# Layer one of a four-layer decoder trunk: VectorE's deferrable work gathered into one list, worked off at three places of each unit

## The chip, the cores and the metric

The kernel runs on one core of a Trainium2 chip. The metric is the device time of one launch in microseconds, lower is better. Five engines work side by side and meet only at semaphores: TensorE (PE; PEld is its weight load), VectorE (DVE), ScalarE (ACT), GpSimd (POOL) and SyncE (SP), which here only issues the weight loads.

## The reference

The input x has 256 positions of 1024 numbers, all float32. Four layers follow one another, each with a mixer of its own: `h = h + rms_norm(mixer(rms_norm(h)))`. The change touches the first, native sparse attention, with 16 query heads, 4 groups of keys, and head width 64:

```python
q, kc, vc, ks, vs, kw, vw, gl, z = split_cols(u @ w_in, A_SPLITS)
kcmp, vcmp = compress(kc, pos_k, w1_k, w2_k), compress(vc, pos_v, w1_v, w2_v)   # gelu(blocks @ w1) @ w2
p_c = masked_softmax(q . kcmp - slope * dist);  o_c = p_c . vcmp    # 15 compressed blocks
p_s = masked_softmax(q . ks   - slope * dist);  o_s = p_s . vs      # top 16 of 4 blocks: all of them
p_w = masked_softmax(q . kw   - slope * dist);  o_w = p_w . vw      # window 512 > 256: all causal keys
o = g_c * o_c + g_s * o_s + g_w * o_w                               # sigmoid gates
return (o * silu(z)) @ w_out
```

With 256 positions the selected and the window branch are both plain causal attention, over different keys and values.

## The kernel before

**Weights.** All weights stream in one order, `seq`, in pieces of up to 512 KB. Each piece is loaded by SP into one of five buffers (`raw`, NS = 5), then split into two float32r parts: a high part (`whi`, a rounded copy by ACT, L133) and a low part (`wlo`, raw minus high, by DVE, L72). A projection is three matmuls per 128 rows: high by high, low of the activations by high, high by low of the weights (L226 to L228). Up to eleven pairs of parts are alive (NH = 11): when the queue's steps are done with a piece, `free` and `advance` let the next piece be split. Below, pieces go by their place in `seq`: 16 and 17 are the first group's queries (called q0), 18 to 25 the compression's w1 (not split), 26 and 27 q1, 28 and 29 z0, 30 and 31 q2, 32 and 33 z1, 34 and 35 q3, 36 and 37 z2, 38 and 39 z3, 40 to 47 the output projection, 48 on the next layer. Here z0 to z3 are the four quarters of the gate path.

**A raw buffer comes free only when its low part is done**, so a low part starts the load five pieces further on.

**Whose order counts.** PE runs in the order of the source throughout. From the compression to the end of the first layer's attention (`st["own"]`), DVE does so too; ACT's order is chosen by the scheduler. In that stretch a low part isn't issued at once: `advance` puts it into `low`, and it is issued by `low_parts(1)` at fixed places, or at the latest when a projection step needs it. Other work that can wait goes through `later(n, f)`: it is issued once n more projection steps have been issued (`plan["count"]`), by `overdue`, which is called after each step.

**The compression.** `compress` does four rounds of eight matmuls, each followed by four steps of q0's projection and, after the first three, `low_parts(1)`. It ends with a cubic and a tanh (`cubic`), then `hidden_t` transposes the hidden values, `second_layer` applies w2 and writes the compressed keys `kc` (L738, L739) and values (L747). Nine steps of q1 stand before `hidden_t`, six after it.

**The units.** `nsa_order` writes 63 places in a row: for each pair of heads p = 0 to 7 (a unit) the front of unit p and the back of unit p-1 in turn. Each unit's places are: `cmp_front` (even p: scores against compressed keys and their reduction L793); `first` (scores of the first 128 queries for both heads, four softmax passes L325 on DVE, then the scaling of the unit before, `scale`, L865 and L871, mixed with five small operations of the compressed branch); `second` (scores of the other 128 queries of head 0, two passes L325); `cmp_back` (odd p); `trans(0)` and `trans(1)` (six transposes L332 each, of unit p-1, copied out by ACT, L172); `finish` (the second queries of head 1, two passes L325); `pvs` (products with the values for unit p-1). After each place `fill` issues projection steps from the queue: two per place up to unit 3, one per place after that; each step is three matmuls. `need(g)` issues steps until group g's queries are there.

The scores sit in two PSUM buffers (`S`, NSB = 2). The second queries of head 0 take the buffer of the first queries of head 0, and so on in turn, so that each score matmul (L846, L847) waits for the DVE pass L325 that read the same buffer before.

**The gate.** `have_z` runs tanh on ACT and then L434 on DVE (`later(6)`), `have_o(p)` calls `go`, which multiplies a quarter of the output by it (L385), and `split` makes its parts (L393, L394) for the output projection.

Of the kernel before, what the change touches and what calls it, by code (L numbers as in the profile page):

```python
# [10 lines left out]
F32 = mybir.dt.float32  # L11
# [4 lines left out]
OP = mybir.AluOpType  # L16
# [7 lines left out]
NH, NS = 11, 5  # L24
LATE, LATEZ, EARLY = -250, -60, 80
NMM, NSB = 3, 2
KO = (0, 4, 1, 5, 2, 6, 3, 7)
X1AT, SUMAT, UAT, T1AT, WARM = 4, 1, 3, 4, 12
POOLED = (6,)
# [8 lines left out]
def trunk(ctx, tc, I, out):  # L38
# [11 lines left out]
    seq = []  # L50
# [11 lines left out]
    for n in "bcd":  # L62
        add(n + "_v", *range(8))
        add(n + "_t", *range(20 if n == "c" else 24))
        add(n + "_o", *range(8))
    st = {"load": 0, "split": 0, "next": 0, "held": 0, "parts": 0, "after": [], "most": len(seq), "own": False}
    raw, parts, low = {}, {}, {}
    waiting = deque()

# [8 lines left out]
    def low_parts(n):  # L78

        for i in sorted(low)[:n]:  # L80
            low.pop(i)()

    def later(n, f):

        if st["own"]:
            waiting.append((plan["count"] + n, f))
        else:
            f()

    def overdue(everything=False):  # L90
        due = [w for w in waiting if everything or w[0] <= plan["count"]]
        for w in due:
            waiting.remove(w)
            w[1]()
        if due:
            overdue(everything)

    def advance(most=len(seq)):
        while True:
# [141 lines left out]
    def pop():  # L241
        fq.popleft()()
        plan["count"] += 1
        overdue()
# [6 lines left out]
    def need(i):  # L251

        while fq and (i not in ready or plan["count"] < ready[i] + 6):
            pop()

    def push_proj(use, q=fq, idx=None):

# [96 lines left out]
    class Gate:  # L354
# [18 lines left out]

        def have_o(self, p):
            self.o.add(p)
            self.go()

        def go(self):
            while self.ready < 4:
# [297 lines left out]
    def keep_q(o, g):  # L677


        for j in range(2):  # L680
            r, other = HALF[j], HALF[1 - j]
            hs = slice(4 * g + j, 4 * g + j + 3, 2)
            hi, sc = t["q"][r, hs, :], cq[r, 2 * g:2 * g + 1]
            with tc.high_priority(offset=EARLY):
                ACT.activation(hi, o[r], AF.Copy, scale=sc)
            later(5, lambda r=r, other=other, hs=hs, hi=hi, sc=sc: DVE.scalar_tensor_tensor(
                t["q"][other, hs, :], o[r], sc, hi.bitcast(F32), op0=OP.mult, op1=OP.subtract))
        ready[g] = plan["count"]

    t = {}  # L690
    W1 = []

    def compress(q, lp):
        if q == 0 and lp == 0:
            t["h"] = ps.tile([128, 256], F32, name="o", bufs=1)
        for kv in range(2):
            PE.matmul(t["h"][64 * kv:64 * kv + 64, :], blkT[:, kv, 4 * q + lp, :], parts[W1[q][kv]][:, lp, :],  # L697
                      start=(q == 0 and lp == 0), stop=(q == 3 and lp == 3))
        if lp == 3:
            free(*W1[q])  # L700
            advance()
        if q == 3 and lp == 3:
            t["q"] = big.tile([128, 16, 256], F32R, name="qT")
            hp = t["h"]
            hid = t["hid"] = work.tile([128, 384], F32, name="P", bufs=8)[:, 0:256]
            ht = work.tile([128, 384], F32, name="P", bufs=8)[:, 0:256]
            ACT.activation(ht, hp, AF.Square)

            def cubic():
                DVE.tensor_scalar(ht, ht, 0.044715, 1.0, op0=OP.mult, op1=OP.add)  # L710
                DVE.tensor_tensor(ht, ht, hp, op=OP.mult)
                ACT.activation(ht, ht, AF.Tanh, scale=math.sqrt(2.0 / math.pi))
                later(3, lambda: DVE.scalar_tensor_tensor(hid, ht, 1.0, hp, op0=OP.add, op1=OP.mult))

            later(1, cubic)
# [16 lines left out]
    def second_layer():  # L732
        kp = ps.tile([128, 512], F32, name="S", bufs=NSB)
        for k in range(2):
            PE.matmul(kp[:, 0:60], w2[:, 0, k].rearrange("p a b -> p (a b)"), t["hk"][:, k, :],
                      start=k == 0, stop=k == 1)
        kp4 = kp[:, 0:60].rearrange("p (g n) -> p g n", g=4)
        ACT.activation(kc[:, :, 0, 0:15], kp4, AF.Copy, scale=0.5)  # L738
        DVE.scalar_tensor_tensor(kc[:, :, 1, 0:15], kp4, 0.5, kc[:, :, 0, 0:15].bitcast(F32), op0=OP.mult,  # L739
                                 op1=OP.subtract)  # L740
        vp = ps.tile([128, 256], F32, name="o", bufs=1)
        for g in range(4):
            for k in range(2):
                PE.matmul(vp[0:60, g * 64:(g + 1) * 64], t["hv"][:, k, g].rearrange("p a b -> p (a b)"),
                          w2[:, 1, k, 0, :], start=k == 0, stop=k == 1)
        for g in range(4):
            DVE.tensor_tensor(vbd[g], vp[0:60, None, g * 64:(g + 1) * 64].to_broadcast([60, 4, 64]),  # L747
                              bm[:, :, None].to_broadcast([60, 4, 64]), op=OP.mult)
# [79 lines left out]
    def nsa_unit(p):  # L828
        g, i = divmod(p, 2)
        t = {}  # L830

        def start():
            need(g)
            t["P"] = {(j, br): work.tile([128, 384], F32, name="P", bufs=8) for j in range(2) for br in range(2)}
            t["l"], t["mx"] = small(8, "la", 3), small(8, "mxa", 3)

        def scores_of(b, js):
            if b == 0:
                start()
            n = 128 * (b + 1)  # L840
            S = {}
            for j in js:
                s = ps.tile([128, 512], F32, name="S", bufs=NSB)
                s = s[:, 0:2 * n].rearrange("p (a n) -> p a n", a=2)
                q = qT[:, 2 * p + j, b * 128:(b + 1) * 128]
                PE.matmul(s, q, KH[:, g, :, 0:n], start=True, stop=False)  # L846
                PE.matmul(s, q, KL[g // 2][:, g % 2, :, 0:n], start=False, stop=True)  # L847
                S[j] = s
            for j in js:
                for br in range(2):  # L850
                    x = (j * 2 + br) * 2 + b
                    softmax(S[j][:, br, :], causal[i], SLA[4 * g + j], 128 * b, 128 * b + n, t["P"][j, br],
                            t["mx"][:, x:x + 1], t["l"][:, x:x + 1])

        def finish():
            scores_of(1, (1,))
            low_parts(1)
            SCALE.append(scale())

        def scale():  # L860
            l = t["l"]
            gv = bass.AP(tensor=gate.tensor, offset=gate.offset + 16 + 2 * p,
                         ap=[list(gate.ap[0]), [1, 2], [16, 2], [48, 2]])
            l4 = l.rearrange("p (j r b) -> p j r b", j=2, r=2)
            ops = [lambda: DVE.reciprocal(l, l), lambda: DVE.tensor_tensor(l4, l4, gv, op=OP.mult)]  # L865
            for br in range(2):
                for j in range(2):
                    x = (j * 2 + br) * 2
                    for b in range(2):
                        P = t["P"][j, br][:, 128 * b:128 * b + 128 * (b + 1)]  # L870
                        ops.append(lambda P=P, x=x + b: DVE.tensor_scalar(P, P, l[:, x:x + 1], None, op0=OP.mult))  # L871
            return ops

        def trans(br):
            t["PT", br] = [transpose_p(t["P"][j, br], "a") for j in range(2)]

        def pv(br):
            if br == 0:
                t["o"] = ps.tile([128, 256], F32, name="o", bufs=1)
            o = t["o"]  # L880
            pv_pair(o, t["PT", br], v, (br * 256 + g * 64,) * 2, br == 0, False)

        def pvs():
            pv(0)
            pv(1)
            o = t["o"]
            for j in range(2):
                PE.matmul(o[64 * j:64 * j + 64, :], vbd[g][:, 2 * i + j, :], PTC[g], start=False, stop=True)
            evac(ga.oT[:, p, :], o, "a")
            ga.have_o(p)  # L890

        def first():
            scores_of(0, (0, 1))
            mixed(*(x.pop(0) for x in (SCALE, CHALF) if x))

        def second():
            scores_of(1, (0,))
            if CHALF:
                mixed(CHALF.pop(0))
            low_parts(1)  # L900

        front = [first, second, finish]
        back = [lambda: trans(0), lambda: trans(1), pvs]
        return front, back

    def nsa_order():
        units = [nsa_unit(p) for p in range(8)] + [([lambda: mixed(SCALE.pop()), *[lambda: None] * 2], None)]
        order = []
        for p in range(9):
            f, b = units[p][0], units[p - 1][1] if p else [lambda: None] * 3  # L910
            if p < 8 and p % 2 == 0:
                order.append(lambda p=p: cmp_front(p // 2))
            order += f[:2]
# [4 lines left out]
                order.append(ga.open)  # L918
        return order

    gh = run(nsa_order(), ga)
    low_parts(len(seq))
    st["own"] = False
    own.close()
# [328 lines left out]
```

## Time and profile before

| | |
|---|---|
| median of 3 runs | 579.8 us (578.29 to 580.72) |
| the profiled execution | 579.91 us, span 578.2 us |
| granted TensorE clock, mean | 0.995 |
| PE busy | 559.3 us, 97% |
| DVE busy | 418.6 us, 72% |
| ACT busy | 335.0 us, 58% |
| the chain that ended last | PE 80%, DVE 9%, issue 5% |

The profile shows one execution. Times in its rows run from the start of the span. A row of the timeline has its start, its length, the engine, the line, the operation, what it writes and reads, and in brackets how long the engine stood idle before it and who released it. A PE matmul's length is a model: back-to-back matmuls start 0.12 us apart and show 0.28. L72's 1.22 us on DVE likewise overlaps its neighbour by some 0.08, so that it takes 1.14 of the engine's time. The units stand between 71 and 158 us.

### The profile page before, as it was taken

Reading aid. Unit: us, or ns where it says so; the run is one execution under the profiler, and the core shown is the slowest. Engines: PE = TensorE matmul, PEld = TensorE weight load, DVE = VectorE, ACT = ScalarE, POOL = GpSimd, SP = SyncE. Lnnn points to the kernel's source line nnn. Section 1 sums busy time; section 2 is a strip of 40 time slices with the busy share of each in tenths; the row PEclk is TensorE's granted clock in tenths of the full one; section 3 lists DMA queues with packets and bytes.
Section 4 is the critical chain, followed back from the end, with each engine's and each line's share of the span. In section 5 each row is a group of like instructions: output and inputs, shape, how many; then the busy total and the mean of one; then the engine's idle time right before and its main releaser. Section 6 shows DMA issues by size and latency. Waiting matters only on the chain.

```text
span 578.2 us, 10454 instructions
## 1 busy us (share of the span) xinstructions
PE 559.3 (97%) x3930; PEld 495.3 (86%) x3930; DVE 418.6 (72%) x927; ACT 335.0 (58%) x719; POOL 41.9 (7%) x89
## 2 busy tenths in 40 slices
PE   7999989999999999999999999999999999999995
PEld 6997878777788799999988789999987898899984
DVE  5883696898857886777965887758548878788632
ACT  6742678788825466567643474757524855666410
POOL 1900000000101100000410100000001000000000
PEclk9999989999999999999999999999999999999999
DMA  9774632322444596443451577443525784332012
GB/s 294 259 246 152 249 110 75 129 91 86 144 154 147 177 332 210 147 147 110 146 158 62 183 270 275 150 143 117 176 73 183 257 289 140 120 108 73 2 37 73
DMA packets 27779, 90.96 MB, mean 157 GB/s; under 512 B 4560, under 2 KB 5200, under 8 KB 27728
## 3 DMA queue, kind: packets, MB, share of 16 engines
q1 hardware_dynamic: 26144, 86.09, 44.2%
q10 hardware_dynamic: 1584, 4.20, 2.3%
q8 instruction: 31, 0.51, 0.4%
q14 instruction: 20, 0.16, 0.1%
HBM read 89.22 MB, written 1.05 MB: 156 GB/s over the span
## 4 chain that ended last, share of the span: by engine, by line
PE 80%; DVE 9%; issue 5%; ACT 2%; POOL 1%; DMA 1%; SPq 0%; POOLq 0%; DVEq 0%; ACTq 0%
PE mm L226 15%; PE mm L227 14%; PE mm L228 14%; PE mm L293 7%; PE mm L292 7%; PE mm L291 7%; DVE wlo L72 4%; PE S L342 3%; PE pt L332 3%; PE o L348 2%; PE o L697 1%; DVE P L325 1%; PE pt L214 1%; DMA h<-in_x_dram 1%; ACT whi L133 1%
## 5 line engine op out<-in xcount | busy, mean ns | idle before, releaser
L226 PE MATMUL mm<-uth,whi 128*128 128x256 f32 x736 | 217.9, 296 | 0.0
L72 DVE TENSOR_TENSOR wlo<-raw,whi 128x1024 fp32r<-128x1024 f32 (+1 forms) x153 | 182.0, 1206 | 41.6 <-ACT whi L133 41.1
L227 PE MATMUL mm<-utl,whi 128*128 128x256 f32 x736 | 208.1, 283 | 0.0
L228 PE MATMUL mm<-uth,wlo 128*128 128x256 f32 x736 | 208.1, 283 | 0.0
L133 ACT ACTIVATE whi<-raw 128x1024 fp32r<-128x1024 f32 (+1 forms) x153 | 156.9, 1044 | 65.9 <-PE mm L227 33.2
L226 PEld LDWEIGHTS mm<-uth,whi 128*128 128x128 f32 x736 | 140.8, 191 | 14.2 <-issue 13.3
L227 PEld LDWEIGHTS mm<-utl,whi 128*128 128x128 f32 x736 | 141.0, 192 | 0.9
L228 PEld LDWEIGHTS mm<-uth,wlo 128*128 128x128 f32 x736 | 140.7, 191 | 0.0
L291 PE MATMUL mm<-whi,qT 128*128 128x512 f32 x128 | 50.4, 394 | 0.0
L292 PE MATMUL mm<-whi,kT 128*128 128x512 f32 x128 | 49.9, 390 | 0.0
L293 PE MATMUL mm<-wlo,qT 128*128 128x512 f32 x128 | 49.9, 390 | 0.0
L291 PE MATMUL mm<-whi,uth 128*128 128x512 f32 (+1 forms) x112 | 42.5, 380 | 0.0
L293 PE MATMUL mm<-wlo,uth 128*128 128x512 f32 (+1 forms) x112 | 42.1, 376 | 0.0
L292 PE MATMUL mm<-whi,utl 128*128 128x512 f32 (+1 forms) x112 | 42.0, 375 | 0.0
L327 ACT ACTIVATE P<-P,mxa 128x128 f32<-128x128 f32 (+1 forms) x64 | 28.4, 446 | 10.6 <-DVE mxa L325 10.5
L325 DVE CUSTOM_DVE_ANT_0 P<-S,mask 128x128 f32<-128x128 f32 (+1 forms) x96 | 29.1, 352 | 7.4 <-PE S L847 5.1
L456 ACT ACTIVATE junk<-mm 128x512 bf16<-128x512 f32 x16 | 9.5, 595 | 42.7 <-PE mm L293 42.7
L332 PE MATMUL pt<-ident,P 128*128 128x128 f32 x180 | 28.3, 280 | 1.7 <-ACT PT L172 0.8
L172 ACT ACTIVATE PT<-pt 128x384 f32<-128x384 f32 x58 | 26.1, 482 | 4.1 <-PE pt L332 3.7
L293 PEld LDWEIGHTS mm<-wlo,qT 128*128 128x128 f32 x128 | 24.0, 188 | 5.0
L291 PEld LDWEIGHTS mm<-whi,qT 128*128 128x128 f32 x128 | 24.1, 188 | 4.7
L292 PEld LDWEIGHTS mm<-whi,kT 128*128 128x128 f32 x128 | 24.1, 188 | 4.7
(206 smaller groups left out, 748.5 us busy)
## 6 DMA issues: line engine op xcount, KB each, us to landing
raw<-in_a_t_dram SPq DMA_DIRECT2D x24, 512.0 KB, 4.4
raw<-in_b_t_dram SPq DMA_DIRECT2D x24, 512.0 KB, 5.0
raw<-in_d_t_dram SPq DMA_DIRECT2D x24, 512.0 KB, 4.6
raw<-in_c_t_dram SPq DMA_DIRECT2D x20, 512.0 KB, 5.6
raw<-in_w_dram SPq DMA_DIRECT2D x8, 512.0 KB, 4.8
raw<-in_a_o_dram SPq DMA_DIRECT2D x8, 512.0 KB, 3.4
raw<-in_b_v_dram SPq DMA_DIRECT2D x8, 512.0 KB, 5.9
raw<-in_b_o_dram SPq DMA_DIRECT2D x8, 512.0 KB, 3.5
```

Of the source, the lines that this page charges most:

```text
L72: lo_of = (POOL if on_pool else DVE).tensor_tensor(lo, t, hi.bitcast(F32), op=OP.subtract)
L133: ACT.activation(hi, t, AF.Copy)
L172: ACT.activation(dst, src, AF.Copy)
L226: PE.matmul(o, sh, mh, start=first, stop=False)
L227: PE.matmul(o, sh, ml, start=False, stop=False)
L228: PE.matmul(o, sl, mh, start=False, stop=last)
L291: PE.matmul(o, sh, wh[:, j, c0:c1], start=k == 0, stop=False)
L292: PE.matmul(o, sl, wh[:, j, c0:c1], start=False, stop=False)
L293: PE.matmul(o, sh, wl[:, j, c0:c1], start=False, stop=k == 7)
L325: DVE.tensor_tensor_reduce(out=P[:, c0:c1], in0=S, in1=mask[:, c0:c1], scale=-slope, scalar=BIG, op0=OP.add, op1=OP.min, accum_out=mx)
L327: ACT.activation(P[:, c0:c1], P[:, c0:c1], AF.Exp, bias=mx, scale=-1.0, accum_out=l)
L332: PE.transpose(pt[:, i, :], P[:, i * 128:(i + 1) * 128], ident)
```

## The change

While the units run, `overdue` issues nothing any more. What is due and the low parts are issued by a new function, `chores(us)`, at three places of each unit: in `trans(0)` (after its transposes and their copies; budget 2.3), in `trans(1)` (likewise; 1.6) and in `finish` (after its two passes L325; 1.2). It takes what is due first, oldest first, at 0.7 each, then low parts at 1.15 each, until the budget is used up or nothing is left; the last item may overrun the budget. Unit 0 has no back, and calls the first two at the same places. `low_parts(1)` goes from `second` and `finish`. `need(g)` now also issues what waits under group g (its queries' low parts L686), and `have_o` calls `go` through `later(2)`. Two more low parts are issued in the compression: one after the tanh in `cubic`, one after L739 in `second_layer`. No computation is added or taken away.

```diff
+U0, U1, U2 = 2.3, 1.6, 1.2
...
-    def later(n, f):
+    def later(n, f, tag=None):
         if st["own"]:
-            waiting.append((plan["count"] + n, f))
+            waiting.append((plan["count"] + n, f, tag))
...
-        due = [w for w in waiting if everything or w[0] <= plan["count"]]
+        due = [w for w in waiting if everything or w[0] <= plan["count"] and not st["units"]]
...
+    def chores(us):
+        while us > 0:
+            due = [w for w in waiting if w[0] <= plan["count"]]
+            if due:
+                waiting.remove(due[0])
+                due[0][1]()
+                us -= 0.7
+            elif low:
+                low_parts(1)
+                us -= 1.15
+            else:
+                return
...
     def need(i):
         while fq and (i not in ready or plan["count"] < ready[i] + 6):
             pop()
+        for w in [w for w in waiting if w[2] == i]:
+            waiting.remove(w)
+            w[1]()
...
         def have_o(self, p):
             self.o.add(p)
-            self.go()
+            later(2, self.go)
...
             later(5, lambda r=r, other=other, hs=hs, hi=hi, sc=sc: DVE.scalar_tensor_tensor(
-                t["q"][other, hs, :], o[r], sc, hi.bitcast(F32), op0=OP.mult, op1=OP.subtract))
+                t["q"][other, hs, :], o[r], sc, hi.bitcast(F32), op0=OP.mult, op1=OP.subtract), g)
...
                 ACT.activation(ht, ht, AF.Tanh, scale=math.sqrt(2.0 / math.pi))
+                low_parts(1)
                 later(3, lambda: DVE.scalar_tensor_tensor(hid, ht, 1.0, hp, op0=OP.add, op1=OP.mult))
...
                                  op1=OP.subtract)
+        low_parts(1)
         vp = ps.tile([128, 256], F32, name="o", bufs=1)
...
         def finish():
             scores_of(1, (1,))
-            low_parts(1)
+            chores(U2)
             SCALE.append(scale())
...
         def trans(br):
             t["PT", br] = [transpose_p(t["P"][j, br], "a") for j in range(2)]
+            chores((U0, U1)[br])
...
         def second():
             scores_of(1, (0,))
             if CHALF:
                 mixed(CHALF.pop(0))
-            low_parts(1)
...
-            f, b = units[p][0], units[p - 1][1] if p else [lambda: None] * 3
+            f, b = units[p][0], units[p - 1][1] if p else [lambda: chores(U0), lambda: chores(U1), lambda: None]
...
+    st["units"] = True
     gh = run(nsa_order(), ga)
+    st["units"] = False
```

## Rows read from the trace of the kernel before

**Rows 1.** Windows: length, then busy time of PE, PEld, DVE, ACT, POOL; granted clock; DMA.

```profile
70.00:80.00 10.00, 7.62 (x57) 7.02 (x56) 9.65 (x36) 6.37 (x18) 0.00 (x0) 1.00 0.28 96
80.00:90.00 10.00, 9.52 (x66) 8.69 (x68) 8.02 (x32) 8.36 (x27) 0.00 (x0) 0.83 0.37 129
...
81.20:84.50 3.30, 3.00 (x13) 2.54 (x12) 3.23 (x19) 2.21 (x7) 0.00 (x0) 0.50 0.47 159
```

**Rows 2.** Waits from 71 to 158 us: who waited for whom, total, times, longest.

```profile
DVE P L325 <- PE S L847: 5.1, 6, 1.9
DVE cs L793 <- PE S L789: 4.8, 3, 2.5
PE S L846 <- DVE mxa L325: 4.3, 5, 2.1
...
PEld pt L332 <- ACT PT L172: 2.4, 7, 0.6
PEld pt L332 <- DVE P L871: 2.3, 8, 0.3
```

**Rows 3.** Timeline of PE around the start of unit 1.

```profile
77.77 0.28 PE L847 MATMUL S<-tu,qT 128*128 128x256 f32 x1
80.18 0.36 PE L846 MATMUL S<-kT,qT 128*128 128x256 f32 x1 [2.13 <-DVE mxa L325]
...
81.74 0.77 PE L846 MATMUL S<-kT,qT 128*128 128x512 f32 x1 [0.30 <-DVE mxa L325]
```

**Rows 4.** Timeline of DVE, unit 0 to the first pass of unit 1.

```profile
71.31 1.21 DVE L72 TENSOR_TENSOR wlo<-raw,whi 128x1024 fp32r<-128x1024 f32 x1
72.44 0.28 DVE L325 CUSTOM_DVE_ANT_0 P<-S,mask 128x128 f32<-128x128 f32 x1
...
76.46 1.22 DVE L72 TENSOR_TENSOR wlo<-raw,whi 128x1024 fp32r<-128x1024 f32 x1
77.71 1.51 DVE L686 SCALAR_TENSOR_TENSOR qT<-mm,cq,qT 64x512 fp32r<-64x512 f32 x2
79.26 0.42 DVE L325 CUSTOM_DVE_ANT_0 P<-S,mask 128x256 f32<-128x256 f32 x1
...
79.95 1.22 DVE L72 TENSOR_TENSOR wlo<-raw,whi 128x1024 fp32r<-128x1024 f32 x1
81.09 0.28 DVE L325 CUSTOM_DVE_ANT_0 P<-S,mask 128x128 f32<-128x128 f32 x1
```

**Rows 5.** Groups of DVE's instructions from 71 to 158 us, shapes apart.

```profile
L72 DVE TENSOR_TENSOR wlo<-raw,whi 128x1024 fp32r<-128x1024 f32 x17 | 20.7, 1219 | 0.0
```

**Rows 6.** Waits of SP's own queue from 71 to 158 us.

```profile
SPq L112 <- DVE wlo L72: 89.8, 18, 14.1
```

**Rows 7.** Timeline of DVE at the end of the compression.

```profile
64.27 0.42 DVE L713 SCALAR_TENSOR_TENSOR P<-P,o 128x256 f32<-128x256 f32 x1 [1.14 <-ACT P L712]
...
66.27 1.23 DVE L72 TENSOR_TENSOR wlo<-raw,whi 128x1024 fp32r<-128x1024 f32 x1
67.52 0.28 DVE L724 COPY P<-pt 128x120 f32<-128x120 f32 x1
...
69.66 1.41 DVE L747 TENSOR_TENSOR v<-o,bm 60x256 f32<-60x256 f32 x4 [0.63 <-PE o L744]
```

**Rows 8.** Timeline of DVE, end of unit 2 and first pass of unit 3.

```profile
103.27 1.22 DVE L72 TENSOR_TENSOR wlo<-raw,whi 128x1024 fp32r<-128x1024 f32 x1
104.41 0.68 DVE L385 SCALAR_TENSOR_TENSOR oT<-oT,zw 128x512 f32<-128x512 f32 x1
105.01 0.28 DVE L325 CUSTOM_DVE_ANT_0 P<-S,mask 128x128 f32<-128x128 f32 x1
```

**Rows 9.** Timeline of PE, the second queries' scores of units 3 and 5.

```profile
105.66 0.47 PE L846 MATMUL S<-kT,qT 128*128 128x512 f32 x1 [0.80 <-DVE mxa L325]
...
125.76 0.47 PE L846 MATMUL S<-kT,qT 128*128 128x512 f32 x1 [0.62 <-DVE mxa L325]
```

**Rows 10.** Timeline of ACT in unit 5.

```profile
127.36 1.05 ACT L133 ACTIVATE whi<-raw 128x1024 fp32r<-128x1024 f32 x1
128.31 0.84 ACT L172 ACTIVATE PT<-pt 128x384 f32<-128x384 f32 x2
```

More of the change, by code (lines that the diff above doesn't have):

```diff
@@ L65, in trunk @@
         add(n + "_o", *range(8))
-    st = {"load": 0, "split": 0, "next": 0, "held": 0, "parts": 0, "after": [], "most": len(seq), "own": False}
+    st = {"load": 0, "split": 0, "next": 0, "held": 0, "parts": 0, "after": [], "most": len(seq), "own": False, "units": False}
     raw, parts, low = {}, {}, {}
```

## The prediction

> **What bounds the kernel now.** I read the split by engine, then a table of ten-microsecond windows over the layer that changes, then the waits in it, then the timelines of PE and DVE where the waits lie. PE is busy 97% of the span, so whatever DVE's new order is worth must appear as PE waiting less or more. In most of the kernel PE has no gap. In the units it has: 2.4 us of the window from 70 to 80 and 0.5 of the next [rows 1], and in that next window the granted clock averages 0.83, because for some 3.3 us it stands at 0.50, 1.2 instead of 2.4 GHz [rows 1]. The waits say for whom: scores for a DVE pass L325 that frees their PSUM buffer, 4.3 us in five waits, transposes for ACT's copies and DVE's scaling, 2.4 and 2.3 us [rows 2]. Over half of the 4.3 us is one place, the start of unit 1: PE issues its last score matmul at 77.77, stands 2.13 us, then 0.30 us again before 81.74 [rows 3]. DVE meanwhile has no gap: a low part at 76.46, q1's two L686, the passes of `finish`, one more low part at 79.95, and only then unit 1's first pass at 81.09 [rows 4]. DVE runs in source order, so these items themselves are what PE waits for. Elsewhere DVE waits for PE as well, 5.1 and 4.8 us [rows 2]. Neither engine is the bound of the whole stretch; the question is at which places DVE's deferrable work stands.
>
> **Part 1, how much is issued where.** Nothing is added, so the cost of the change is in positions. A low part takes 1.14 us of DVE: 79.95 to 81.09 [rows 4]; 17 of them fill 20.7 us [rows 5]. Before, each unit issues two, one in `second` and one in `finish`. Now follow the budgets. When unit 0 reaches `trans(0)`, pieces 26 and 27 are used up, so eleven pairs 28 to 38 have been split in the source's order. With pieces 28 and 29 done in the compression, 30 to 38 wait in `low`. `trans(0)`: q1's two L686 are due, 2.3 - 1.4 = 0.9 is left, one low part (30). `trans(1)`: 1.6 pays for one and 0.45 is left, so a second (31, 32). `finish`: 1.2 - 1.15 = 0.05 is left, so again two (33, 34). Unit 1 likewise: two, then z0's L434 and one, then two: 35 to 39. After that the list is short, since a piece is split only when one eleven places earlier is done: three in unit 2 (40 to 42), two in unit 3, then one per unit. The counts are 5, 5, 3, 2, 1, 1, 1, 1 where there were 2 each.
>
> Would units 0 and 1 find nothing to do because the loads are late? SP's queue waits 89.8 us for low parts in 18 waits [rows 6]: buffers are full and loads wait for DVE, not DVE for loads. I take no stall from that in units 0 to 2.
>
> **Part 2, the compression.** Low part 28 moves from 66.27 into the 1.14 us that DVE stands before L713, low part 29 from 71.31 to before L747, which waits 0.63 us itself [rows 4, 7]. In the first case L713 can slip by 0 to 1.14 us, and the transposes of the hidden values with it, but L724 no longer stands behind 1.25 us of L72 [rows 7]: the two about cancel on PE. In the second 1.14 us leaves the front of unit 0's first pass (72.44) and about half of it comes back through L747. I take -0.5 us for that pass, with 0 and -1.1 as ends.
>
> **Part 3, unit 0 and the start of unit 1.** Between the passes of `second` and unit 1's first pass stand three more low parts: 32, 33, 34. That is 3 x 1.14 = 3.4 us on an engine without a gap there [rows 4]. With -0.5 unit 1's first pass goes from 81.09 to 84.0, and PE's scores for its second queries from 81.74 to about 84.6, +2.9 us. The wait of 2.13 us grows by about 1.8 (two low parts ahead of the passes of `finish`, less 0.5), the one of 0.30 takes the rest. Nothing covers this: unit 0 has no back, so PE has only six projection matmuls to put between. The bounds are +2.3 and +3.4.
>
> **Part 4, the clock.** Before, PE worked at half clock from 81.74 to about 84.5, and lost half of that, 1.4 us [rows 1, 3]. After the change the stops before 84.6 are longer (about 4 and 2 us, where the row showed 2.13 and 0.30), so I expect at least one half-clock stretch to fall behind 84.6 too and cost the same 1.4: no change. If the clock is back by then, -1.4; if it stays low through unit 1, twice the price, +1.4. The Trainium skill ("TensorE: Matmul & The Clock Gate", HAM oscillation) says that a stop long enough sends the clock back to half and that the next work starts cold each time, with a loss of half the throttled time. By that rule the loss per stop would be an estimated 1.65 us from a stretch of 3.3 us, and the sum 0.25 higher; the trace agrees that one stop was followed by one such stretch.
>
> **Part 5, unit 2.** Before its successor's first pass DVE did two low parts, two L686 and L385; the last low part and L385 are shown [rows 8]. Now there are three low parts and two L686, and L385 moves to unit 3: 1.14 - 0.6 = +0.5 us, again in front of a score that PE already waits 0.80 us for [rows 9]. The end below is 0, if PE is the later one there by then; above, 1.14.
>
> **Part 6, units 3 to 7.** What comes back is at most what PE still waits for here. The low part and L385 that stood before unit 5's first pass are gone from there, and a low part from before unit 7's: the wait of 0.62 [rows 9] and about 0.1 in unit 7, -0.7. Of the 2.3 us of waits for scaling [rows 2] most follow an even unit's scores at once, where DVE was already idle for PE, so I take -0.2. ACT's high parts cause some of the 2.4 us for its copies: one ran from 127.36 and the copy followed it at 128.31 [rows 10]. Fewer high parts are made here, so I take -0.5, between 0 and -1.4. Sum -1.4. Against it stands a new wait: with `low` run dry, a low part is issued as soon as its piece is split, and DVE, in order, then waits for ACT's high part with the passes of `finish` behind it, and PE's next scores behind these. I count it at 0, with up to +2 as an end (a high part of 1.05 us behind a copy and an exponential or two, in two units).
>
> **The sum.** Against the profiled execution's 579.91 (0.1 above the median of 579.8): +2.9, 0, +0.5, -1.4, together +2.0: 581.9, with 582.0 as the forecast. This is 0.4% above and so inside the 0.5%, 2.9 us, that a measurement of this kernel can about tell from no change.
>
> **The rivals.** *The early low parts pay later.* If all the other PE waits fall away (4.3, 2.4 and 2.3 us [rows 2] less the 2.4 of unit 1's start [rows 3], 6.6) and the clock is back at 84.6, the sum is 2.9 - 1.4 + 0.5 - 6.6 = -4.6: 575.3. For it speaks that later units have one low part instead of two; against it, that half of these waits have other causes than low parts. *About even:* the recovery is 3 instead of 1.4, 580.3; for it speaks that DVE is six low parts, 7 us, ahead after unit 1. *The clock stays low through unit 1*, which ends on the other side: PE loses 2.8 instead of 1.4 after 84.6 and the sum is +3.4, 583.3. It decides from the point where the half-clock stretches reach past about 87 us. For it speaks the doubled standstill, against it that one stop of 2.13 cost one stretch only; the page named in part 4 is on its side. *DVE waits for ACT's high parts* in units 3 to 7: +2, 583.9; for it, that the list is empty there; against it, that a unit 5 or 7 has 0.5 to 1.5 us of slack.
>
> **How the numbers follow.** The forecast with 580.6 to 582.8 gets 0.33, about even 0.17, the faster rival 0.13, the clock 0.20, the wait for high parts 0.17. Faster by over 0.5% is the first rival, 0.13; slower is the last two, 0.37; within, 0.50. The range leaves out the far end of the faster rival and both mishaps of the slower side together: 577.8 to 585.2.
>
> **What would show it.** In the profile after: five low parts L72 between the first pass of unit 0 and that of unit 1, PE's wait there of about 4 us with a second of about 2, DVE without a gap to unit 2; granted clock in the window from 80 to 90 at 0.83 or below. In units 4 to 7 one L72 each, and the wait before unit 5's second scores gone. The prediction is wrong if unit 1's first pass isn't later than 83, if the stall is made good in unit 1 (then DVE wasn't the bound there), or if DVE's waits for ACT's high parts appear with more than 2 us.

## The result: 592.85 us, 2.3% slower, and the profile after

The changed kernel takes 592.85 us (592.05 to 593.1, 4 runs) against 579.68 before; the ratio is 1.0226 with a 95% interval from 1.0203 to 1.025. The forecast was 582.0 in a range up to 585.2, so the loss of 13.2 us is five to six times the one expected. The profiled execution took 592.75 with a span of 591.0. In the changed kernel lines have moved: DVE's pass is L344 (before: L325), its low part L73 (L72), its query part L705 (L686), its scaling L892 (L871), its gate product L404 (L385); ACT's high part is L149 (L133); PE's scores are L867 and L868 (L846, L847), its compressed scores L810 (L789), its transposes L351 (L332).

Outside the first layer's units nothing has changed. Here is the start of each unit, the first score matmul of its `first`, and the last matmul of unit 7 (L888, in the changed kernel L910), from the profiles' timelines, in us:

| | 0 | 1 | 2 | 3 | 4 | 5 | 6 | 7 | end |
|---|---|---|---|---|---|---|---|---|---|
| before | 71.2 | 77.6 | 93.7 | 103.5 | 115.6 | 124.2 | 135.4 | 144.0 | 158.3 |
| after | 71.0 | 77.2 | 98.5 | 109.3 | 121.6 | 130.2 | 144.0 | 153.5 | 171.1 |
| difference | -0.2 | -0.4 | +4.8 | +5.8 | +6.0 | +6.0 | +8.6 | +9.5 | +12.8 |

The 12.8 us at the end are the 12.8 of the two spans. Unit 1 starts 0.4 us earlier than before; 5.2 us are lost in unit 1, 1.2 in units 2 and 3, nothing in unit 4, 2.6 in unit 5, 0.9 in unit 6 and 3.3 in unit 7. First the windows of the changed kernel, with the columns of [rows 1]:

```profile
70.00:80.00 10.00, 7.37 (x56) 6.79 (x55) 9.16 (x31) 5.75 (x17) 0.00 (x0) 1.00 0.17 52
80.00:90.00 10.00, 7.03 (x29) 6.54 (x30) 9.90 (x32) 6.56 (x18) 0.00 (x0) 0.55 0.80 265
90.00:100.00 10.00, 10.00 (x81) 8.89 (x80) 6.89 (x20) 8.59 (x21) 0.00 (x0) 0.94 0.78 250
140.00:150.00 10.00, 8.27 (x41) 7.98 (x42) 7.52 (x38) 5.13 (x17) 0.00 (x0) 0.66 0.18 54
160.00:170.00 10.00, 7.48 (x52) 5.93 (x50) 7.17 (x23) 6.00 (x15) 1.15 (x4) 0.83 0.17 54
```

The granted clock, the column after POOL's, sags three times where it had sagged once: 0.55, 0.66, 0.83. In each of these windows PE also has its fewest matmuls. The waits from 71 to 172 us, to be read against [rows 2]:

```profile
PE S L867 <- DVE mxa L344: 6.4, 4, 4.7
DVE wlo L73 <- ACT whi L149: 6.0, 3, 3.3
DVE P L344 <- PE S L868: 5.4, 7, 1.8
...
DVE cs L814 <- PE S L810: 3.1, 3, 1.4
...
PE pt L351 <- DVE P L892: 2.5, 1, 2.5
PE S L810 <- DVE qT L705: 2.4, 2, 1.9
```

PE's waits for a pass rose from 4.3 to 6.4 us. Three rows have no counterpart in [rows 2]: DVE waits 6.0 us for ACT's high parts, PE 2.4 us for L705 and 2.5 in one piece for the scaling. The timeline of PE around these stops, against [rows 3]:

```profile
77.35 0.28 PE L868 MATMUL S<-tu,qT 128*128 128x256 f32 x1
82.33 0.55 PE L867 MATMUL S<-kT,qT 128*128 128x256 f32 x1 [4.71 <-DVE mxa L344]
...
85.02 0.76 PE L867 MATMUL S<-kT,qT 128*128 128x512 f32 x1 [0.64 <-DVE mxa L344]
...
139.02 0.28 PE L244 MATMUL mm<-uth,wlo 128*128 128x256 f32 x1
141.23 0.28 PE L810 MATMUL S<-kc,qT 128*128 128x32 f32 x1 [1.93 <-DVE qT L705]
142.02 1.34 PE L810 MATMUL S<-kc,qT 128*128 128x32 f32 x7 [0.50 <-DVE qT L705]
...
162.66 0.28 PE L244 MATMUL mm<-uth,wlo 128*128 128x256 f32 x1
165.46 1.16 PE L351 MATMUL pt<-ident,P 128*128 128x128 f32 x6 [2.52 <-DVE P L892]
...
170.84 0.65 PE L910 MATMUL o<-PTc,v 60*64 60x256 f32 x4
```

And DVE's at the same three places, the first against [rows 4], and in unit 3 (119.03):

```profile
76.34 1.51 DVE L705 SCALAR_TENSOR_TENSOR qT<-mm,cq,qT 64x512 fp32r<-64x512 f32 x2
77.88 3.50 DVE L73 TENSOR_TENSOR wlo<-raw,whi 128x1024 fp32r<-128x1024 f32 x3
81.41 0.42 DVE L344 CUSTOM_DVE_ANT_0 P<-S,mask 128x256 f32<-128x256 f32 x1
...
82.10 2.35 DVE L73 TENSOR_TENSOR wlo<-raw,whi 128x1024 fp32r<-128x1024 f32 x2
84.38 0.28 DVE L344 CUSTOM_DVE_ANT_0 P<-S,mask 128x128 f32<-128x128 f32 x1
...
119.03 1.23 DVE L73 TENSOR_TENSOR wlo<-raw,whi 128x1024 fp32r<-128x1024 f32 x1 [2.09 <-ACT whi L149]
...
134.47 0.69 DVE L404 SCALAR_TENSOR_TENSOR oT<-oT,zw 128x512 f32<-128x512 f32 x1
138.49 1.22 DVE L73 TENSOR_TENSOR wlo<-raw,whi 128x1024 fp32r<-128x1024 f32 x1 [3.33 <-ACT whi L149]
139.63 0.42 DVE L344 CUSTOM_DVE_ANT_0 P<-S,mask 128x256 f32<-128x256 f32 x1
...
140.43 1.53 DVE L705 SCALAR_TENSOR_TENSOR qT<-mm,cq,qT 64x512 fp32r<-64x512 f32 x2
...
159.63 0.23 DVE L963 CUSTOM_DVE_ANT_0 P<-P 128x64 f32<-128x64 f32 x1 [1.82 <-DMA P<-in_b_lambda_dram]
...
161.83 1.23 DVE L73 TENSOR_TENSOR wlo<-raw,whi 128x1024 fp32r<-128x1024 f32 x1 [0.60 <-ACT whi L149]
162.98 0.42 DVE L344 CUSTOM_DVE_ANT_0 P<-S,mask 128x256 f32<-128x256 f32 x1
...
165.03 1.93 DVE L892 TENSOR_SCALAR P<-P,la 128x128 f32<-128x128 f32 x8
```

In unit 0 the five low parts stand where the prediction put them, three ahead of the passes of `finish` and two behind. In unit 5 DVE stands 3.33 us ahead of a single low part, and the passes and then L705 follow it in the queue; PE needs L705 for unit 6's compressed scores. In unit 7 a low part begins at 161.83, the passes at 162.98, and the scaling that PE's last transposes need only at 165.03. The third of the 6.0 us of waits for a high part is in unit 3: 2.09 us, with no L705 behind it, and unit 3 takes only 0.3 us longer than before the change. L705 stood at the same place before the change (there L686), behind the last low part of unit 5, but that low part didn't wait:

```profile
131.31 1.22 DVE L72 TENSOR_TENSOR wlo<-raw,whi 128x1024 fp32r<-128x1024 f32 x1
132.56 1.53 DVE L686 SCALAR_TENSOR_TENSOR qT<-mm,cq,qT 64x512 fp32r<-64x512 f32 x2
```

Why the low part in unit 5 waits is on ACT:

```profile
134.12 1.37 ACT L704 ACTIVATE qT<-mm,cq 64x512 fp32r<-64x512 f32 x2
135.52 0.87 ACT L188 ACTIVATE PT<-pt 128x384 f32<-128x384 f32 x2
136.41 0.51 ACT L346 ACTIVATE P<-P,mxa 128x256 f32<-128x256 f32 x1
136.92 0.49 ACT L346 ACTIVATE P<-P,mxa 128x256 f32<-128x256 f32 x1
137.41 1.04 ACT L149 ACTIVATE whi<-raw 128x1024 fp32r<-128x1024 f32 x1
```

The queries' copies, two copies of transposes and two exponentials run back to back from 134.12, and the high part follows at 137.41. The list on DVE is empty but for this piece.

### The profile page after: what moved, and what is told of

It is laid out like the page before. It is cut to its first block, busy times and chain, and to the rows that moved or that the text cites. A ratio compares the mean times of both kernels' runs of the same rounds, so it can differ in the third digit from the quotient of the medians.

```text
span 591.0 us, 10472 instructions
## 1 busy us (share of the span) xinstructions
PE 565.1 (96%) x3930; PEld 501.8 (85%) x3930; DVE 418.9 (71%) x927; ACT 335.9 (57%) x719; POOL 41.4 (7%) x89
## 3 DMA queue, kind: packets, MB, share of 16 engines
HBM read 89.22 MB, written 1.05 MB: 153 GB/s over the span
## 4 chain that ended last, share of the span: by engine, by line
PE 79%; DVE 8%; ACT 5%; issue 4%; POOL 1%; DMA 1%; SPq 0%; POOLq 0%; DVEq 0%; ACTq 0%
PE mm L242 15%; PE mm L243 14%; PE mm L244 14%; PE mm L311 6%; PE mm L310 6%; PE mm L312 6%; DVE wlo L73 4%; PE S L361 3%; PE pt L351 3%; PE o L367 2%; ACT whi L149 2%; PE o L716 1%; PE pt L230 1%; ACT P L346 1%; DMA h<-in_x_dram 1%
## 5 line engine op out<-in xcount | busy, mean ns | idle before, releaser
L73 DVE TENSOR_TENSOR wlo<-raw,whi 128x1024 fp32r<-128x1024 f32 (+1 forms) x153 | 181.7, 1205 | 48.5 <-ACT whi L149 47.4
L149 ACT ACTIVATE whi<-raw 128x1024 fp32r<-128x1024 f32 (+1 forms) x153 | 156.9, 1044 | 66.8 <-PE mm L243 33.3
L242 PEld LDWEIGHTS mm<-uth,whi 128*128 128x128 f32 x736 | 142.4, 193 | 14.3 <-issue 13.3
L243 PEld LDWEIGHTS mm<-utl,whi 128*128 128x128 f32 x736 | 142.7, 194 | 0.9
L244 PEld LDWEIGHTS mm<-uth,wlo 128*128 128x128 f32 x736 | 142.3, 193 | 0.0
L344 DVE CUSTOM_DVE_ANT_0 P<-S,mask 128x128 f32<-128x128 f32 (+1 forms) x96 | 29.2, 352 | 7.7 <-PE S L868 5.4
L351 PE MATMUL pt<-ident,P 128*128 128x128 f32 x180 | 29.6, 294 | 3.7 <-DVE P L892 2.5
```

Of the source, the lines that this page charges most:

```text
L73: lo_of = (POOL if on_pool else DVE).tensor_tensor(lo, t, hi.bitcast(F32), op=OP.subtract)
L149: ACT.activation(hi, t, AF.Copy)
L242: PE.matmul(o, sh, mh, start=first, stop=False)
L243: PE.matmul(o, sh, ml, start=False, stop=False)
L244: PE.matmul(o, sl, mh, start=False, stop=last)
L344: DVE.tensor_tensor_reduce(out=P[:, c0:c1], in0=S, in1=mask[:, c0:c1], scale=-slope, scalar=BIG, op0=OP.add, op1=OP.min, accum_out=mx)
```

## The experiments

The theory after reading the profile: most of the loss sits at three places, the pile of low parts in unit 0, and the waits for a high part in units 5 and 7, each with its half-clock stretch. The rival: the loss comes from the other half of the edit, holding due work (L705, L404, L453) back to three places. Ratios are to the kernel before, measured on the same chip. Times of single kernels differ between chips by some tenths of a us, and starts of unit 0 in the profiles lie between 71.0 and 72.8, so that stretches between two starts say more than the starts themselves.

**Unit 0 as it was.**

```diff
-            chores(U2)
+            chores(U2 if p else 0.5)
...
-            f, b = units[p][0], units[p - 1][1] if p else [lambda: chores(U0), lambda: chores(U1), lambda: None]
+            f, b = units[p][0], units[p - 1][1] if p else [lambda: chores(1.5), lambda: None, lambda: None]
```

> The changed kernel, with unit 0 issuing what it did before the change: q1's two L705 and one low part ahead of the passes of finish, one low part behind them. My theory (the cost sits at three places: the pile of low parts in unit 0, a wait for ACT's high part in unit 5, the same in unit 7): the pile's 5 to 6 us go, about 1 comes back as the same low parts now crowd units 2 and 3, so 587 to 589. The rival (the cost is in the held due work, L705, L404 and L453, not in the low parts): 592 to 593.

Measured: 591.65 us (590.5 to 591.96), ratio 1.0189 [1.0172, 1.0206]. The theory's 587 to 589 was wrong. Unit 2 now starts at 93.1 (before 93.7), but unit 4 at 120.7 (before 115.6). The budgets of units 2 and 3 take what unit 0 left, four low parts in a row ahead of the passes of `finish`, and PE waits there, as its timeline shows:

```profile
103.71 0.28 PE L867 MATMUL S<-kT,qT 128*128 128x256 f32 x1
106.56 0.36 PE L867 MATMUL S<-kT,qT 128*128 128x256 f32 x1 [2.45 <-DVE mxa L344]
108.65 0.77 PE L867 MATMUL S<-kT,qT 128*128 128x512 f32 x1 [0.61 <-DVE mxa L344]
```

So a pile isn't a matter of unit 0. It forms where the budgets meet a full list: from the start of unit 3 to that of unit 4 this kernel takes 17.0 us where the kernel before took 12.0, about what the pile in unit 0 costs in the changed kernel.

**A reserve of two.** A low part is taken from the list only while more than two wait.

```diff
-            elif low:
+            elif len(low) > 2:
```

> The changed kernel, with a low part issued from the list only while more than two wait there, so that DVE never reaches one whose high part ACT is still to make. My theory: the waits before the compressed scores of unit 6 and before the last transposes go, with their half-clock stretches: minus 5 to 6.5, 586 to 588. The rival (L705 held until the compressed scores need it is what PE waits for, reserve or not): 591 to 593.

Measured: 581.74 us (580.76 to 583.02), ratio 1.0032 [1.0019, 1.0045]. This one condition gives back 11.1 us, more than the theory's 5 to 6.5. The pile in unit 0 is untouched (unit 2 starts at 98.3), but units 6 and 7 now start at 138.0 and 146.6, 2.6 us behind the kernel before instead of 8.6 and 9.5, and the end is at 159.9. Of DVE's waits the row for the high part is gone:

```profile
DVE cs L814 <- PE S L810: 6.4, 3, 2.5
DVE P L344 <- PE S L868: 3.0, 6, 1.1
DVE la L886 <- ACT P L346: 0.9, 1, 0.9
DVE cl L828 <- ACT cs L826: 0.3, 1, 0.3
```

The same edit also leaves one low part fewer in unit 2, and between the starts of units 2 and 4 it needs 21.0 us instead of 23.1, a part of its gain that the theory hadn't counted.

**Both edits.**

```diff
-            elif low:
+            elif len(low) > 2:
...
-            chores(U2)
+            chores(U2 if p else 0.5)
...
-            f, b = units[p][0], units[p - 1][1] if p else [lambda: chores(U0), lambda: chores(U1), lambda: None]
+            f, b = units[p][0], units[p - 1][1] if p else [lambda: chores(1.5), lambda: None, lambda: None]
```

> Both of the edits before. My theory: they add, 581 to 584. The rival of held due work: above 590.

Measured: 583.99 us (582.42 to 584.66), ratio 1.0057 [1.0037, 1.0077]. The time lies at the edge of the theory's range, but the theory was wrong: the edits don't add (the two gains, 1.2 and 11.1 us, would give 580.5). The pile of units 2 and 3 comes back as in the first experiment: unit 4 starts at 121.1.

**PE kept busy in the first stop.** Between the two score matmuls of unit 1:

```diff
+                if p == 1 and b == 0 and j == 1:
+                    warm = ps.tile([128, 256], F32, name="o", bufs=1)
+                    for _ in range(18):
+                        PE.matmul(warm[:, 0:128], ident, ident, start=True, stop=True)
                 s = ps.tile([128, 512], F32, name="S", bufs=NSB)
```

> The changed kernel plus 18 matmuls without use (identity by identity into a PSUM buffer that nobody reads) in unit 1 ahead of the score matmul that waits 4.9 us, so that PE isn't idle there; they fit into the wait. If the half-clock stretch from 81 to 91 us costs time of its own: minus 2 to 4, 589 to 591. If DVE, busy 99% from 80 to 90, sets the pace there whatever the clock: 592 to 593.

Measured: 592.57 us (589.99 to 593.7), ratio 1.0205 [1.017, 1.0241]. The clock stays up through the pile:

```profile
70.00:80.00 10.00, 9.74 (x79) 9.37 (x79) 9.17 (x32) 6.03 (x17) 0.00 (x0) 1.00 0.16 54
80.00:90.00 10.00, 7.16 (x55) 6.30 (x53) 9.90 (x32) 6.42 (x18) 0.00 (x0) 1.00 0.76 263
```

DVE is busy 9.90 of the 10 us in both kernels. Unit 1's second scores begin 7.79 us after its first in both, so up to there DVE sets the pace whatever the clock. From these scores to the start of unit 2 this profile shows 12.22 us, that of the changed kernel 13.46. The half clock as such isn't the reason: the kernel of the next experiment has the same code up to unit 4 and the same stop of 4.71 us, and in its profile this way takes 12.28 us, though it does show the half clock, for a shorter time (0.50 from 82.4 to 89.0, against 81.0 to 91.2 in the changed kernel):

```profile
80.00:90.00 10.00, 6.58 (x31) 6.09 (x32) 9.90 (x32) 6.29 (x17) 0.00 (x0) 0.66 0.77 265
```

Three later profiles of the same code (without a low part in unit 5, in units 5 and 7, and the last experiment), with 0.66 to 0.69 in that window, show 12.5 to 12.9. So behind this stop a half clock of less than 7 us cost 0.1 to 0.7 us, and the 10.2 us in the changed kernel's profile some 1.2. In the medians nothing can be told: these four runs spread over 3.7 us.

**L705 ahead of the low part that waits.**

```diff
-            later(5, lambda r=r, other=other, hs=hs, hi=hi, sc=sc: DVE.scalar_tensor_tensor(
+            later(1 if g == 3 else 5, lambda r=r, other=other, hs=hs, hi=hi, sc=sc: DVE.scalar_tensor_tensor(
```

> The changed kernel with the last group's two L705 due four steps earlier, so that in unit 5 they stand ahead of the low part that waits for ACT's high part, instead of behind it. If PE's 2.8 us stop before unit 6's compressed scores is L705 held up behind that wait: the stop and the half-clock stretch after it go, minus 3 to 4, 589 to 590. If any DVE delay there stops PE, L705 or not (the passes of finish are as late as before): minus 1 at most.

Measured: 587.71 us (587.67 to 588.99), ratio 1.015 [1.0131, 1.0168], so 5.1 us less than the changed kernel, more than the 3 to 4 expected. The low part still waits for its high part (1.43 us), but L705 stands before it, and PE's compressed scores run without a stop; unit 6 starts at 139.9 instead of 144.0:

```profile
134.79 1.53 DVE L705 SCALAR_TENSOR_TENSOR qT<-mm,cq,qT 64x512 fp32r<-64x512 f32 x2 [0.37 <-ACT qT L704]
137.76 1.23 DVE L73 TENSOR_TENSOR wlo<-raw,whi 128x1024 fp32r<-128x1024 f32 x1 [1.43 <-ACT whi L149]
```

What PE waited for in unit 6 is L705, and what L705 waited for is the low part ahead of it.

**No low part late in unit 5; in units 5 and 7.** `chores` gets a switch that leaves low parts out at `trans(1)` and `finish` of the units named; they follow in the next. The diff is that of the second run; the first names unit 5 alone.

```diff
-    def chores(us):
+    def chores(us, lows=True):
...
-            elif low:
+            elif low and lows:
...
-            chores((U0, U1)[br])
+            chores((U0, U1)[br], br == 0 or p + 1 not in (5, 7))
...
-            chores(U2)
+            chores(U2, p not in (5, 7))
```

> The changed kernel without a low part at unit 5's places trans(1) and finish (it is issued in unit 6 instead). My theory: unit 6 starts 2.5 to 3.5 us earlier against the changed kernel, the stop at unit 7's end stays: 588.5 to 590. Rival (the loss is spread, and what is gained here is waited out later): 591 to 593.

Measured: 588.46 us (587.29 to 590.52), ratio 1.0159 [1.0134, 1.0184]. From the start of unit 5 to that of unit 7 its profile shows 18.80 us where the changed kernel took 23.27.

> The same in units 5 and 7. My theory: another 3 us from the stop before the last transposes, 585 to 587, and the rest to the kernel with a reserve (581.7) lies in units 2 and 3. Rival: as with unit 5 alone.

Measured: 583.34 us (583.09 to 584.46), ratio 1.0071 [1.0055, 1.0086], a larger gain than the theory's 585 to 587. So the low part in unit 5 costs 4.4 us (592.85 to 588.46) and the one in unit 7 another 5.1. With two low parts moved out of a late place, 9.5 of the 13.2 us are back.

**Due work as before.** The condition on `st["units"]` is taken out of `overdue`; only low parts go through `chores`.

```diff
-        due = [w for w in waiting if everything or w[0] <= plan["count"] and not st["units"]]
+        due = [w for w in waiting if everything or w[0] <= plan["count"]]
```

> The changed kernel, but what is due is issued after each step as before the change, and only low parts go through the three places. My theory: the low parts still run dry, so within 2 us of the changed kernel, 591 to 595. The rival of held due work: near the kernel with a reserve or better, below 584.

Measured: 591.99 us (591.55 to 592.6), ratio 1.0217 [1.0202, 1.0232]. DVE waits 7.6 us for high parts. The rival falls: holding due work back isn't the main cause, and L705 stands behind the waiting low part here too (at 139.46, PE waits 1.9 us for it). A small price of its own isn't excluded, since without due work the first budgets take four low parts in a row in unit 0 instead of three, and PE's stop there is 5.83 us long.

**The compression alone**, on the kernel before: `low_parts(1)` after the tanh and after L739, nothing else.

```diff
                 ACT.activation(ht, ht, AF.Tanh, scale=math.sqrt(2.0 / math.pi))
+                low_parts(1)
...
                                  op1=OP.subtract)
+        low_parts(1)
         vp = ps.tile([128, 256], F32, name="o", bufs=1)
```

> The kernel before with nothing but the two extra low parts in the compression. The prediction's part 2 gives unit 0's first pass 0.5 us earlier, with 0 and 1.1 as ends, and the units as before: 578.7 to 579.8, so not to be told from no change, or faster by 0.2%. Rival: L713 slips, and PE with it, by up to 1 us: 580 to 581.

Measured: 579.58 us (578.37 to 581.13), ratio 0.9998 [0.9985, 1.0011]. Unit 0's first pass starts at 71.49 instead of 72.44 and 0.3 us are left at the end of the units. No change that can be told.

**A falling reserve**: seven low parts stay in the list at first, two in unit 7, with the budgets unchanged.

```diff
+KEEP = (7, 7, 6, 6, 5, 4, 3, 2, 2)
...
-            elif low:
+            elif len(low) > KEEP[p]:
```

> The changed kernel with its budgets, but with a reserve that starts at seven low parts and falls to two in unit 7, so that neither unit 0 gets a pile nor a late unit runs dry. My theory: between the kernel with a reserve of two less its 4.6 us of unit 0, 577 to 580. Rival (taking the due work at three places has a price of its own): 581 or more.

Measured: 583.51 us (582.72 to 584.29), ratio 1.0066 [1.005, 1.0083]. The theory's 577 to 580 was wrong, the rival's number right, though not shown to be for the rival's reason: three low parts still fall into unit 0 (unit 2 starts at 95.7), and eight of them into units 4 to 7 where the first reserve had four. DVE waits 2.2 us for high parts again.

**A table.** One low part ahead of the passes of `finish` (two in unit 1), none behind them in even units, and due work only in odd units and at the end:

```diff
+LOWS = ((1, 0, 0), (1, 1, 1), (1, 0, 0), (1, 0, 2), (1, 0, 0), (1, 0, 1), (1, 0, 0), (1, 0, 0), (0, 3, 0))
...
-    def chores(us):
+    def chores(p, k):
+        for w in [w for w in waiting if w[0] <= plan["count"] and (p % 2 or p == 8)]:
+            waiting.remove(w)
+            w[1]()
+        low_parts(LOWS[p][k])
```

> The low parts by a table, one ahead of the passes of finish in every unit, the rest behind these passes in units 1, 3 and 5 alone, where DVE waited for PE, and due work only in odd units. No low part stands ahead of an odd unit's first pass. My theory: PE's waits for a DVE pass at units 1, 3, 5 and 7 (4.3 us before) shrink to about one, 576 to 578. Rival: what is taken from one pass delays the next, 579 to 581.

Measured: 577.27 us (576.42 to 580.84, 11 runs), ratio 0.9964 [0.9948, 0.998]: faster than both kernels, by 2.3 us against the one before, as the theory said. In its profile unit 1's stop is short, the clock is at 1.00 from 80 to 90, and PE waits 0.7 us for passes instead of 4.3:

```profile
PE S L860 <- DVE mxa L337: 0.7, 1, 0.7
```

What the places of the low parts and what the held due work have to do with it each was not separated.

**The next layer's small operations held back.** In unit 7 DVE waited 1.82 us for a load on behalf of L963, of the next layer. The edit puts L963 to L967 under `tc.issue_after(st["lo"])`.

```diff
+    with tc.issue_after(st["lo"]):
+        for i in range(2):
+            DVE.tensor_tensor_reduce(out=ljunk, in0=lamt[:, 2 * i, :], in1=lamt[:, 2 * i + 1, :], scale=1.0,
...
+        DVE.tensor_scalar(lam[:, 3:4], lam[:, 2:3], -LI, None, op0=OP.add)
```

> The changed kernel with the next layer's four small lambda operations on DVE, which wait 1.8 us for a load in unit 7 ahead of its last low part, held back until the first layer's low parts are done. If the stop at unit 7's end comes from that load: minus 2.5 to 4, 589 to 590. If the low part waits for ACT's high part anyway (160.73 to 161.80, on an ACT that has no gap before it), the DVE operations only stood in that wait: 592 to 593, and DVE's wait for a high part grows from 0.6 to about 4 us there.

Measured: 592.38 us (590.72 to 593.63), ratio 1.0231 [1.0214, 1.0248]: no gain. DVE now waits for the high part alone:

```profile
156.84 0.42 DVE L344 CUSTOM_DVE_ANT_0 P<-S,mask 128x256 f32<-128x256 f32 x1
161.18 1.22 DVE L73 TENSOR_TENSOR wlo<-raw,whi 128x1024 fp32r<-128x1024 f32 x1 [3.92 <-ACT whi L149]
```

So the row of 0.60 us in the changed kernel hid a wait of 3.9. Other work had been put into it, and its own wait was named in its place.

The profile shows a second thing. PE's stop ahead of the last transposes is as long as in the changed kernel (2.45 us, there 2.52), but no half clock follows it. The granted clock is 1.00 in the window where it was 0.83, and from the transposes to the last products of unit 7 the same matmuls take 4.00 us instead of 5.38:

```profile
160.00:170.00 10.00, 7.55 (x63) 5.56 (x60) 7.42 (x20) 6.26 (x14) 1.16 (x4) 1.00 0.17 54
164.81 1.07 PE L351 MATMUL pt<-ident,P 128*128 128x128 f32 x6 [2.45 <-DVE P L892]
...
168.81 0.65 PE L910 MATMUL o<-PTc,v 60*64 60x256 f32 x4
```

So here the half clock cost 1.4 us. Whether the edit kept it away isn't shown: this execution took 590.72 us, the other three of this kernel 592.21 to 593.63.

## Why the prediction was wrong

*The bound.* Right in the main: PE's time is lost only in the units, at waits for DVE, and in part in the half-clock stretches behind them.

*Part 1, the counts.* Right: three and two low parts in unit 0, and one per unit from unit 4 on, are in the trace. That the first of them don't wait for loads was right as well: DVE is busy 9.90 of 10 us.

*Part 2.* Unit 0's first pass came 0.90 us earlier (71.54 against 72.44), within the ends given (0 to 1.1, taken 0.5). No effect on the time that could be told, by the run with the compression alone.

*Part 3.* Right in mechanism and nearly in size: unit 1's second scores at 85.02 against 81.74, +3.3 where +2.9 was said. The first wait grew to 4.71 (said: about 4), the second is 0.64 (about 2). From there to unit 2 another 1.5 us were lost that the sum didn't have (13.46 us where 11.93 were taken before). Up to 1.2 of them are the half clock that lasted to 91.2 in this execution: without it, and with a shorter one, the same way took 12.22 and 12.28 us. That DVE would have no gap up to unit 2 didn't come true: it waits 1.17 and 1.25 us for PE there.

*Part 4.* No change was said, with +1.4 if the clock stayed low through unit 1. In the changed kernel's profile it stayed low for 10.2 us instead of 3.3, past the 87 us at which the rival was to decide, and cost about the 1.2 us just named; in other executions of the same code it stayed low for less than 7 us and cost 0.1 to 0.7. The Trainium skill ("TensorE: Matmul & The Clock Gate", HAM oscillation) says that a stop long enough sends the clock back to half, and the trace agrees (0.55 in the window from 80 to 90, with the stop of 4.71 us). By the loss rule that the Trainium skill gives there, half of the throttled time, the 10.2 us behind the first stop would cost an estimated 5.1 us and the 3.4 us behind the last one an estimated 1.7. The traces show 1.2 and 1.4: far less than the rule where DVE set the pace, and nearly as much where PE did.

*Part 5.* The term was right: +0.5 was said, and unit 3's second scores begin 2.66 us after its first where it was 2.14. But 1.0 us more lies between the starts of units 2 and 3 (93.7 to 103.5, then 98.5 to 109.3), at the transposes of unit 2, whose second six wait 0.69 us for ACT's copies. The sum didn't have that.

*Part 6 is the step that failed*, and in it one sentence: of the new wait for ACT's high part, "I count it at 0, with up to +2 as an end (a high part of 1.05 us behind a copy and an exponential or two, in two units)". The units and the mechanism were right. Taking the two low parts out of their places in units 5 and 7 gives 9.5 us back. The prediction's own sign of being wrong, more than 2 us of waits for high parts, was there: 6.0. Two things were mis-sized. First, what stands ahead of the high part on ACT: six operations for 3.3 us in unit 5, and 3.9 us of waiting in unit 7 when nothing else fills it. I had allowed for two or three. Second, what is queued behind on DVE. I gave the wait the slack of the passes of `finish`; but q3's two L705 stand behind the low part and these passes, and PE needs them for unit 6's compressed scores at once. In the kernel before they ended at 134.09, and the compressed scores began at 134.06: there was no slack. Moving L705 alone is worth 5.1 us. In unit 7 it is the scaling for the last transposes, with no more projection steps for PE to do meanwhile. After each of these stops the granted clock fell again (0.66 and 0.83 in the windows above), and the prediction had no price for that. It is 1.4 us in unit 7, as the last experiment's profile shows. For units 5 and 6 an estimate of about 2 is left: 23.27 against 18.80 us, less the stops of 1.93 and 0.50; the clock stands at 0.50 there from 142.4 to 149.2, with PE busy throughout.

The recovery that part 6 counted at -1.4 can't be read from the changed kernel itself, where the stops cover most of it (that unit 5's second scores no longer wait, 0.62 before, can be). In the profile without the two low parts unit 5 takes 10.2 us where it took 11.2 before, the way from unit 7's start to its last product 13.5 instead of 14.0, and units 4 and 6 the same as before: about -1.5.

With the failed term out of the kernel, the run without the two low parts takes 583.34 us, and the one with a reserve 581.74: inside the range, near the forecast of 582.0. The rival named *DVE waits for ACT's high parts* was the true one, with a price of +2 where it was +9.5. What spoke for it, an empty list, could be read from the counts 2, 1, 1, 1, 1.

Not settled: why the falling reserve takes 583.5 and not less (against the kernel before its profile loses 1.9 us up to unit 2, 0.7 in units 2 and 3, 0.5 in unit 5 and 0.7 in unit 7), and why unit 2's transposes wait for ACT in the changed kernel.

## What to carry to other kernels

A list of deferrable work needs a floor as well as a budget. DVE worked off its list in order here; with the list empty, the next item was the one whose input ACT was just making, and everything behind it waited too. One condition, to leave two items in the list, was worth 11 us. Ask what stands behind an item that may wait, and how soon another engine needs it: a wait of 2.09 us with no L705 behind it moved the next unit by 0.3 us at most, one of 3.33 us with L705 behind it cost 4.4. And spread the items by where the engine waits for others (here odd units, behind the passes of `finish`), not by equal budgets: a table that does so, with the same work, made the kernel 0.36% faster than before.

## What was not expected of the hardware

The half clock has no fixed price. Behind the first stop, with DVE busy 9.90 of 10 us, 6.6 us of it cost 0.1 (up to 0.7 in other executions) and 10.2 us some 1.2; behind the last stop, with PE at work throughout, 3.4 us of it cost 1.4. Nor does the length of a stop alone say whether it comes: one of 2.13 us was followed by it in the kernel before, one of 2.45 us in the last experiment was not. And an idle row names only the last releaser: the wait for a high part showed as 0.60 us with other work in it and as 3.92 us when that work was moved away.
